# Differential q, k, v as twelve feature-major tiles of the dense stage ahead of the RWKV scan, in place of token-major products beside it

## The chip, the cores and the metric

One core of a Trainium2 chip runs the whole kernel. The metric is the device time of one execution in microseconds (us); the figure for a kernel is the median of its runs.

## The reference, cut to what matters

Two layers run over 640 tokens (512 latent tokens on a grid 64 wide, 128 context tokens) with 1024 features. The first layer mixes tokens by MLA and a retention, the second by differential attention and a bidirectional RWKV-7 recurrence; a gated feed-forward network with a short convolution follows each. The change is in the second layer:

```python
def odd_inputs(h, po):
    w_in, qn, kn = po[:3]
    b, n, _ = h.shape
    dq, dk, dv, p = split_cols(h @ w_in, ODD_SIZES)
    q = rms_norm(dq.reshape(b, n, DIFF_HEADS, 2, DIFF_DH), qn)
    k = rms_norm(dk.reshape(b, n, DIFF_HEADS, 2, DIFF_DH), kn)
    v = dv.reshape(b, n, DIFF_HEADS, 2 * DIFF_DH)
    rw = rwkv_inputs(p, *po[5:13])
    return q, k, v, rw
```

Here h is the normalised and modulated input. q, k and v have 512 columns each (4 heads, two maps of 64 features), and the columns p of the recurrence another 1920. Latent q and k are rotated (rotary position code on pairs of neighbouring features); the attention of a head takes two softmax maps, subtracts lambda times the second from the first, and multiplies by v. Keys and values of 256 cached context tokens are read beside the new ones. The normalised k and the v of the context tokens are outputs.

## The kernel before

**Dense products.** A feature-major tile is 128 output features by all tokens. `fm_steps` (line 454) makes one from a weight that is split into a high and a low fp32r part and an input that is split in the same way: three products (hi*hi, hi*lo, lo*hi) for each of 8 slices of 128 input features and each of two halves of the columns, 48 in all, recorded on line 470. The weights come in order from a list of jobs: `pump` loads them on SP's queue four jobs ahead and splits them on ACT (line 414) and DVE (line 415). The normalised input is not formed for these tiles: the final x is scaled by the modulation and split, two more columns carry the shifts (so 642 columns, 322 and 320), and `fm_norm` multiplies each product by the rstd `rb` (line 665) and adds the shift (line 666).

**The dense stage of the odd layer.** `rwkv_in` runs 15 such tiles for the recurrence in the order `RW_ORDER`. After each tile DVE and ACT form the token shift; four tiles are turned to token-major on TensorE (line 1583), four pass through a gate product (line 1534), and `rwkv_kk` makes a head norm of four of them with `head_sums` (lines 770 and 775), `head_rows` (line 794) and `head_bcast` (line 804). Beside eight of the tiles, lines 1552 and 1554 form the normalised h itself, in place in the eight x tiles, in fp32, for the differential q, k, v. The true x was spilled to DRAM before.

**The scan.** `rwkv_scan` handles five groups of a forward and a backward chunk of 128 tokens. `pre` prepares a group (lines 1791 to 1875), `lb` and `lc` solve its triangular leaves (lines 1890 to 1948), `steps` advances the state (lines 1971 to 2014). `weave` emits them together: first `pre(0)`; then `pre(1)` with the leaves of group 0; then, five times, the steps of group g with `pre(g+2)` and the leaves of g+1. Between their events a background stream is advanced; `BG` gives how many of its steps go into each of these seven parts, and `Side.step` lets no TensorE instruction of the stream go ahead of what the main streams issued a few events before. A scheduler of the framework then sets the order on each engine.

**The background stream.** `side_mix` runs `odd_qkv` and then `diff_attn`. `odd_qkv` takes six groups of 256 columns: for each of five token tiles 8 fp32 products of 128x128 by 128x256 (line 1325, two records each) from the stored h and token-major weights of 1 MB a group. The results are copied and squared on ACT, normalised, multiplied by the gain and rotated on DVE and POOL, turned by two transposes (line 1303), split (lines 440 and 444) into one buffer and stored to DRAM. It has 121 steps. `diff_attn` has 176: for each of 4 heads `load` issues 14 transfers on POOL's queue (lines 1424 to 1429); then, for each of 5 query tiles and 2 maps, the scores (line 1442) go into one PSUM buffer, and DVE takes the maximum, ACT the exponential (line 1448); then the maps are combined, transposed (line 1467) and multiplied by v (line 1472).

After the scan, `odd_out` reloads x and runs the output projection.

## Time and profile before

| what | value |
|---|---|
| median of 3 runs | 2074.09 us (2069.32 to 2077.87) |
| span of the profiled execution, first to last instruction | 2059.5 us |
| TensorE busy, share of the span | 1952.7 us, 95% |
| VectorE (DVE) busy | 1253.8 us, 61% |
| ScalarE (ACT) busy | 887.3 us, 43% |
| GpSimd (POOL) busy | 186.5 us, 9% |
| instructions | 36275 |

The span runs from the first to the last instruction on the core; the device time of a run has some more around it. Lines named L are lines of the kernel. PE is TensorE's products, PEld its weight loads, SP the engine that issues most DMAs; a q behind an engine's name is its sequencer. PEclk is the granted clock of TensorE as a share of 2.4 GHz, so 0.50 is 1.2 GHz. Records of products overlap, since they are pipelined, so a sum of their lengths is above the time that the engine was busy.

### The profile page before, as it was taken

How to read it: one execution, taken by the hardware profiler on the slowest of the kernel's cores; microseconds unless marked ns; L12 is line 12 of the kernel's file. 1: busy time of each engine (PE TensorE's matmuls, PEld its weight loads, DVE VectorE, ACT ScalarE, POOL GpSimd, SP SyncE). 2: the span in 40 equal slices, each digit the busy share in tenths (PEclk: the TensorE clock that was granted, in tenths of full speed). 3: DMA queues.
4: the chain of work that ended last, by engine and by line, in shares of the span. 5: the costliest groups of instructions: out<-in, count | busy, mean ns of one | idle time of the engine just before them, and what ended most of it. 6: DMA issues, size and time to landing. Idle time of an engine off the chain costs nothing.

```text
span 2059.5 us, 36275 instructions
## 1 busy us (share of the span) xinstructions
PE 1952.7 (95%) x14376; PEld 1765.7 (86%) x14376; DVE 1253.8 (61%) x2752; ACT 887.3 (43%) x1680; POOL 186.5 (9%) x365
## 2 busy tenths in 40 slices
PE   6999999999999999999989897898779999999999
PEld 3998565999899899999978676777679999999999
DVE  6554657556456465577436856877667764656555
ACT  4433344334244243456333334667534542524343
POOL 1001000000000000000024332332110000000000
PEclk9999999999999999999989998979989999999999
DMA  8237344234543512143264554454453212122221
GB/s 323 67 109 242 105 134 163 89 104 147 181 153 116 192 62 83 60 151 104 83 207 100 109 161 120 100 116 96 100 200 106 77 58 92 60 85 67 77 63 71
DMA packets 190676, 243.60 MB, mean 118 GB/s; under 512 B 90730, under 2 KB 132970, under 8 KB 190508
## 3 DMA queue, kind: packets, MB, share of 16 engines
q1 hardware_dynamic: 184880, 225.87, 35.7%
q0 software_dynamic: 3904, 13.37, 2.2%
q8 instruction: 113, 1.85, 0.4%
q10 hardware_dynamic: 1724, 2.06, 0.3%
q14 instruction: 55, 0.45, 0.1%
HBM read 202.05 MB, written 39.21 MB: 117 GB/s over the span
## 4 chain that ended last, share of the span: by engine, by line
PE 81%; DVE 7%; DMA 6%; ACT 3%; issue 2%; POOL 1%; SPq 0%; ACTq 0%; DVEq 0%; POOLq 0%
PE mm L470 59%; PE qkv L1325 2%; PE ada L541 2%; PE rv L913 1%; PE pv L1130 1%; PE mm L1097 1%; DMA dk<-pt 1%; PE ptr L1120 1%; PE sc L1442 1%; DVE X L1902 1%; DVE tmp L1901 1%; DMA xd<-X 1%; DMA mq<-tr 1%; DMA raw<-ada 1%; PE mm L1098 1%
## 5 line engine op out<-in xcount | busy, mean ns | idle before, releaser
L414 ACT CAST hi<-raw 128x1024 fp32r<-128x1024 f32 (+4 forms) x212 | 195.9, 925 | 574.1 <-PE mm L470 528.6
L470 PE MATMUL mm<-hhi,hi 128*128 128x322 f32 x1648 | 381.0, 312 | 0.0
L470 PE MATMUL mm<-hlo,hi 128*128 128x322 f32 x1648 | 380.3, 311 | 0.0
L470 PE MATMUL mm<-hhi,lo 128*128 128x322 f32 x1648 | 380.1, 311 | 0.0
L470 PEld LDWEIGHTS mm<-hhi,hi 128*128 128x128 f32 x1648 | 278.3, 189 | 8.7 <-issue 6.7
L470 PEld LDWEIGHTS mm<-hlo,hi 128*128 128x128 f32 x1648 | 279.5, 190 | 0.0
L470 PEld LDWEIGHTS mm<-hhi,lo 128*128 128x128 f32 x1648 | 278.6, 189 | 0.0
L415 DVE TENSOR_TENSOR lo<-raw,hi 128x1024 fp32r<-128x1024 f32 (+4 forms) x212 | 226.1, 1067 | 58.7 <-ACT hi L414 36.0
L672 DVE SCALAR_TENSOR_TENSOR x<-mm,ada,x 128x512 f32<-128x512 f32 (+1 forms) x176 | 88.7, 545 | 176.1 <-PE mm L470 175.9
L470 PE MATMUL mm<-ahi,hi 128*128 128x320 f32 x704 | 161.7, 311 | 0.0
L470 PE MATMUL mm<-ahi,lo 128*128 128x320 f32 x704 | 160.7, 309 | 0.0
L470 PE MATMUL mm<-alo,hi 128*128 128x320 f32 x704 | 160.3, 309 | 0.0
L663 DVE COPY shv<-mm 128x2 f32<-128x2 f32 x103 | 16.3, 159 | 207.9 <-PE mm L470 207.9
L470 PEld LDWEIGHTS mm<-ahi,hi 128*128 128x128 f32 x704 | 117.1, 188 | 12.0 <-ACT hi L414 10.1
L1325 PE MATMUL qkv<-w,x 128*128 128x256 f32 x480 | 118.9, 402 | 0.1
L470 PEld LDWEIGHTS mm<-ahi,lo 128*128 128x128 f32 x704 | 117.8, 188 | 0.0
L470 PEld LDWEIGHTS mm<-alo,hi 128*128 128x128 f32 x704 | 117.6, 188 | 0.0
L666 ACT ACTIVATE u<-u,shv 128x128 f32<-128x128 f32 (+1 forms) x176 | 90.3, 557 | 48.8 <-DVE u L665 47.0
L734 DVE SCALAR_TENSOR_TENSOR ac<-u,vt,ac 128x642 f32<-128x642 f32 x88 | 78.0, 887 | 52.5 <-ACT ac L732 52.3
L1325 PEld LDWEIGHTS qkv<-w,x 128*128 128x128 f32 x480 | 94.0, 201 | 17.0 <-issue 1.7
L732 ACT ACTIVATE ac<-u,vt 128x642 f32<-128x642 f32 x88 | 81.3, 925 | 2.8
L665 DVE TENSOR_TENSOR u<-mm,rb 128x128 f32<-128x128 f32 (+1 forms) x176 | 77.3, 481 | 2.5 <-ACT rb L650 2.5
(419 smaller groups left out, 3351.3 us busy)
## 6 DMA issues: line engine op xcount, KB each, us to landing
raw<-ada SPq DMA_DIRECT2D x96, 512.0 KB, 4.6
raw<-up SPq DMA_DIRECT2D x88, 512.0 KB, 3.5
raw<-down SPq DMA_DIRECT2D x32, 384.0 KB, 3.1
raw<-down SPq DMA_DIRECT2D x32, 320.0 KB, 2.8
fs<-df SPq DMA_DIRECT2D x10, 832.0 KB, 5.2
raw<-wb_fm SPq DMA_DIRECT2D x15, 512.0 KB, 3.5
w<-wb_tm SPq DMA_DIRECT2D x12, 512.0 KB, 4.5
raw<-wa_fm SPq DMA_DIRECT2D x11, 512.0 KB, 4.3
```

Of the source, the lines that this page charges most:

```text
L414: nc.scalar.copy(hi, t)
L415: nc.vector.tensor_tensor(lo, t, hi.bitcast(F32), op=OP.subtract)
L470: nc.tensor.matmul(ps[:, c0 + b:c0 + e], wt[:, ws], at[:, b:e], start=first and j == 0, stop=last and j == 2)
L541: nc.tensor.matmul(ps[32 * j:32 * j + 32, :], self.cs[:, k, :], pieces[j // 2][:, (j % 2) * 512:(j % 2) * 512 + 512], start=k == 0, stop=k ...
L665: nc.vector.tensor_tensor(u[:, o], ps[:, s], rb[:, s], op=OP.mult)
L666: nc.scalar.activation(u[:, o], u[:, o], AF.Identity, bias=sh[:, c:c + 1])
L672: nc.vector.scalar_tensor_tensor(x[:, s], ps[:, s], self.ada_v(l, part, m, c), x[:, s], op0=OP.mult, op1=OP.add)
L732: nc.scalar.activation(ac, u[:, 1:643], AF.Identity, scale=cv[:, 1, f:f + 1], bias=self.vec(f"cb{l}", f))
L734: nc.vector.scalar_tensor_tensor(ac, u[:, 0:642], cv[:, 0, f:f + 1], ac, op0=OP.mult, op1=OP.add)
L913: nc.tensor.matmul(ps[:, :272], at[:, ts], wt[:, k * 272:k * 272 + 272], start=n == 0, stop=n == 23)
L1097: nc.tensor.matmul(sc[:, 0:512], q, kT[:, 0:4], start=True, stop=True)
L1325: nc.tensor.matmul(ps, h[k][:, t * 128:t * 128 + 128], w[k // 4][:, k % 4 * 256:k % 4 * 256 + 256], start=k == 0, stop=k == 7)
```

## The change

The 12 tiles of q, k and v are appended to the list of feature-major weights (`wb_fm` has 27 tiles in place of 15, and `wb_tm` is gone). A new stage `diff_in` runs them after the 15 tiles of the recurrence, from the same split input, with `fm_plain` in place of `fm_norm` (no padding for a token shift). The columns of q and k are permuted inside each head so that the first and second members of the rotary pairs form halves of 32 features; the rotation needs a copy with these halves swapped, made by four DMAs from SBUF to SBUF for each tile. The head norm uses `head_sums`, `head_rows` and `head_bcast`. `odd_qkv`, the normalised copy of h and its lines 1552 and 1554 are removed. The background stream of the scan is the attention alone, and `BG` is set anew. `diff_attn` reads q, k and the cached k in the new layout.

```diff
-BG = (89, 24, 102, 0, 22, 72, 0)
+BG = (14, 24, 26, 26, 26, 30, 30)
...
     def odd_jobs(self):
-        for m in RW_ORDER:
+        for m in RW_ORDER + tuple(range(15, 27)):
             self.jobs_fm("wb_fm", m)
-
-    def odd_qkv(self, D):
...
-                    for k in range(8):
-                        nc.tensor.matmul(ps, h[k][:, t * 128:t * 128 + 128], w[k // 4][:, k % 4 * 256:k % 4 * 256 + 256], start=k == 0, stop=k == 7)
-                        if k % 2:
-                            next(pp, None)
-                            yield
...
     def odd_in(self, hp):
...
-        with self.pool("wd") as wp:
-            self.rwkv_in(D, wp)
+        with self.pool("rbo") as rp:
+            rb = rp.tile([128, TOK], F32, name="rb")
+            with self.pool("wd") as wp:
+                h = self.rwkv_in(D, wp, rb)
+            with self.pool("qk") as qp:
+                self.diff_in(D, h, rb, qp)
         return D
 
+    def fm_plain(self, h, dst, rb):
+
+        nc = self.nc
+        ps = self.fm_tile(h, [8], TOK + 2)
+        sh = self.sp.tile([128, 2], F32, name=self.nm("shv"), tag="shv", bufs=4)
+        nc.vector.tensor_copy(sh, ps[:, TOK:])
+        nc.vector.tensor_tensor(dst, ps[:, :TOK], rb, op=OP.mult)
+        for c, s in ((0, slice(0, LAT)), (1, slice(LAT, TOK))):
+            nc.scalar.activation(dst[:, s], dst[:, s], AF.Identity, bias=sh[:, c:c + 1])
+
+    def diff_in(self, D, h, rb, qp):
...
+        def post(name, ts):
+            sqs = []
+            for t in ts:
+                sqs.append(self.A("qsq", F32))
+                nc.scalar.activation(sqs[-1], t, AF.Square, scale=0.125)
+            yield
+            r = self.head_sums(sqs, 0, self.MM, al)
+            yield
+            rows = self.head_rows(r, self.MM, al)
+            yield
+            for p, t in enumerate(ts):
+                mm = self.head_bcast(rows, p, self.MM)
+                nc.vector.scalar_tensor_tensor(t, t, self.vec(f"d{name}n"), mm, op0=OP.mult, op1=OP.mult)
+                if name == "k":
+                    nc.sync.dma_start(a["dk_o"][p], t[:, LAT:])
+                sw = qp.tile([128, LAT], F32, name=self.nm("sw"), tag="sw", bufs=2)
+                for i in range(4):
+                    j = i ^ 1
+                    nc.sync.dma_start(sw[32 * i:32 * i + 32], t[32 * j:32 * j + 32, :LAT])
+                yield
+                nc.gpsimd.tensor_tensor(sw, sw, rope[:, 1], op=OP.mult)
+                nc.vector.tensor_tensor(t[:, :LAT], t[:, :LAT], rope[:, 0], op=OP.mult)
+                nc.vector.tensor_tensor(t[:, :LAT], t[:, :LAT], sw, op=OP.add)
+                hl = [qp.tile([128, TOK], F32R, name=self.nm("qhl"), tag="qhl", bufs=4) for _ in range(2)]
+                self.split_to(*hl, t)
+                for n in range(2):
+                    nc.sync.dma_start(D[name][p, n], hl[n].bitcast(F32))
+                yield
+
+        pp = iter(())
+        for name in ("q", "k"):
+            ts = []
+            for p in range(4):
+                t = self.A("dq", F32)
+                self.fm_plain(h, t, rb)
+                ts.append(t)
+                for _ in range(3):
+                    next(pp, None)
+            for _ in pp:
+                pass
+            pp = post(name, ts)
+            next(pp)
+        for p in range(4):
+            d = self.A("dv", F32)
+            self.fm_plain(h, d, rb)
+            for _ in range(3):
+                next(pp, None)
...
     def side_mix(self, D):
-        yield from self.odd_qkv(D)
         with self.pool("at", 1, "left") as ap, self.psum("scp") as scp, self.psum("trp") as trp:
             yield from self.diff_attn(D, ap, scp, trp)
...
-            if 1 < n < 10:
-                k = n - 2
-                t = self.x[k]
-                nc.vector.tensor_tensor(t, t, rb, op=OP.mult)
-                for c, s in ((0, slice(0, LAT)), (1, slice(LAT, TOK))):
-                    nc.scalar.activation(t[:, s], t[:, s], AF.Identity, scale=am[:, k, c:c + 1], bias=self.ada_v(1, 0, k, c))
```

Each v tile is then turned to token-major by five transposes and stored, as the recurrence's v is.

## Rows read from the trace of the kernel before

**Rows 1.** The page: the span, and TensorE's granted clock in 40 slices.

```profile
span 2059.5 us, 36275 instructions
...
PEclk9999999999999999999989998979989999999999
```

**Rows 2.** Busy time by stage: stretch, its length, engines with instruction counts, clock, DMA share, GB/s.

```profile
core 0: us, PE busy (x) PEld busy (x) DVE busy (x) ACT busy (x) POOL busy (x), PEclk, DMA share, GB/s
...
968.00:1038.00 70.00, 70.00 (x472) 69.31 (x471) 34.34 (x74) 26.76 (x51) 2.23 (x4) 1.00 0.33 103
...
1291.00:1361.00 70.00, 61.25 (x709) 50.21 (x707) 53.20 (x172) 44.80 (x117) 22.40 (x37) 0.86 0.50 114
...
1050.00:1232.00 182.00, 170.16 (x1027) 137.05 (x1027) 108.87 (x318) 66.54 (x175) 64.38 (x100) 0.92 0.50 125
1232.00:1505.00 273.00, 230.03 (x2900) 189.10 (x2900) 192.94 (x622) 164.27 (x421) 70.35 (x121) 0.86 0.49 117
```

**Rows 3.** Chain that ended last, 968 to 1062: start us, length us, what.

```profile
974.13 0.55 PE mm L794 x5
974.68 7.18 PE mm L470 x48
981.86 0.29 PE mm L804 x2
...
1018.80 0.55 PE vtr L1583 x5
...
1037.57 0.61 PE mm L470 x4
...
1050.55 2.08 PE lp L1800 x8
```

**Rows 4.** Line 1980, a product of every state step: lengths, first and last start.

```profile
L1980 PE MATMUL pa<-G,zb x320: 218/218/366, 1232.0 to 1502.2; 64*64 64x64 f32 x160
```

**Rows 5.** TensorE's groups, 1043 to 1508: count, busy us, mean ns, idle before.

```profile
L1325 PE MATMUL qkv<-w,x 128*128 128x256 f32 x480 | 118.9, 402 | 0.1
L1472 PE MATMUL pv<-av,wT 128*128 128x128 f32 x200 | 35.1, 337 | 1.1 <-ACT wT L1468 1.1
L1442 PE MATMUL sc<-ak,aq 128*128 128x512 f32 (+1 forms) x80 | 32.3, 481 | 19.7 <-ACT p L1448 19.6
...
L1467 PE MATMUL ptr<-ident,p 128*128 128x128 f32 x100 | 21.9, 333 | 4.7 <-ACT wT L1468 2.8 <-ACT wT L1474 1.9
...
L1442 PE MATMUL sc<-ac,aq 128*128 128x256 f32 x64 | 14.7, 316 | 0.0
```

**Rows 6.** Line 1442, the scores: what TensorE sat idle for before them (us, times).

```profile
  ACT p L1448: 42.0, 32
```

**Rows 7.** Chain that ended last, 950 to 1700: token-major products, sums of squares.

```profile
1064.75 7.10 PE qkv L1325 x32
...
1519.43 1.28 PE mm L770 x16
```

**Rows 8.** Chain that ended last, 915 to 968: the head stage of the recurrence.

```profile
962.09 1.05 ACT hi L414
...
966.21 0.76 PE mm L775 x5
```

**Rows 9.** Line 1554, ACT's part of the normalised h: lengths, first and last start.

```profile
L1554 ACT ACTIVATE x<-x,ada,am x16: 478/646/819, 939.9 to 949.8; 128x512 f32<-128x512 f32 x8, 128x128 f32<-128x128 f32 x8
```

**Rows 10.** Timeline of the handover to the scan; idle before and its releaser in brackets.

```profile
1047.85 0.69 SPq L1314 DMA_DIRECT2D w<-wb_tm  x1
1048.54 0.75 ACT L1584 COPY vt<-vtr 128x512 f32<-128x512 f32 x2 [3.87 <-DMA dvt<-vt]
```

**Rows 11.** Weight loads' groups, 1043 to 1232: the token-major products' loads.

```profile
L1325 PEld LDWEIGHTS qkv<-w,x 128*128 128x128 f32 x480 | 94.0, 201 | 17.0 <-issue 1.7 <-ACT m L1333 0.4 <-DMA w<-wb_tm 0.4
```

**Rows 12.** Busy time of line 1442 alone: PE with count, PEld, clock, DMA.

```profile
1429.00:1484.00 55.00, 11.13 (x40) 7.62 (x40) 0.87 0.47 106
1484.00:1505.00 21.00, 0.88 (x4) 0.59 (x4) 0.99 0.68 214
```

**Rows 13.** Busy time in a stretch of the main part, columns as in rows 2.

```profile
1360.00:1370.00 10.00, 9.56 (x165) 8.45 (x166) 4.16 (x14) 7.46 (x19) 2.49 (x5) 0.50 0.34 88
```

More of the change, by code (lines that the diff above doesn't have):

```diff
@@ L32 @@
     ("qn", 1), ("kn", 1), ("qn1", 1), ("kn1", 1), ("retgn", 4), ("diffgn", 4),
[1 row of a table removed]
[1 row of a table added]
 ]
[L35 removed]
+_ROW = [("qnr", 32), ("knr", 32), ("decay", 8), ("lam", 256)]
 _CST = [("cosm", 128), ("sinm", 128), ("reta", 128), ("retb", 128),
@@ L70, in _rope_tables, with _perm_cols, _rope_fm @@
     return lay(c), lay(s)
+PERM = np.concatenate([np.arange(0, 64, 2), np.arange(1, 64, 2)])
+def _perm_cols(w):
+    return w.reshape(w.shape[0], -1, 64)[:, :, PERM].reshape(w.shape[0], -1)
+def _rope_fm():
+    t = np.arange(LAT)
+    inv = 10000.0 ** (-np.arange(16) / 16)
+    ang = np.concatenate([(t // GRID_W)[:, None] * inv, (t % GRID_W)[:, None] * inv], -1).T
+    c, s = np.cos(ang), np.sin(ang)
+    return np.concatenate([np.tile(c, (4, 1)), np.tile(np.concatenate([-s, s], 0), (2, 1))], 1).astype(np.float32)
 def _consts():
@@ L158, in _layout @@
     put("a0", _fm(a["rwkv_a0"][0]))
+    for s in ("q", "k"):
+        put(f"d{s}n", np.tile(a[f"diff_{s}n"][0][PERM], 2)[:, None])
     o["vec"] = vec
     o["row"] = np.concatenate([
-        a["mla_qn"][0][64:], a["mla_kn"][0][64:], a["diff_qn"][0], a["diff_kn"][0],
+        a["mla_qn"][0][64:], a["mla_kn"][0][64:],
         a["ret_decay"][0].reshape(-1), a["diff_lam"][0].reshape(-1)])[None].astype(np.float32)
@@ new lines, in diff_in @@
+    def diff_in(self, D, h, rb, qp):
+        nc, a = self.nc, self.a
+        rope = qp.tile([128, 2, LAT], F32, name="ropd")
+        nc.scalar.dma_start(rope.rearrange("p a t -> p (a t)"), a["ropd"])
+        kc = self.W("kc", 1024)
+        nc.scalar.dma_start(kc, a["dkc"])
+        for n, x in enumerate(self.split_wide(kc)):
+            nc.sync.dma_start(D["kc"][:, n].rearrange("h p x -> p h x"), x.bitcast(F32).rearrange("p (h x) -> p h x", h=4))
+        al = lambda dt: self.A("hr", dt)
+        def post(name, ts):
[44 more added lines that the diff above has]
+                next(pp, None)
+            vt = qp.tile([128, TOK], F32, name=self.nm("dvt"), tag="dvt", bufs=2)
+            for t0, t1 in ((0, 4), (4, 5)):
+                tp = self.PS("vtr")
+                for t in range(t0, t1):
+                    nc.tensor.transpose(tp[:, (t - t0) * 128:(t - t0) * 128 + 128], d[:, t * 128:t * 128 + 128], self.ident)
+                nc.scalar.copy(vt[:, t0 * 128:t1 * 128], tp[:, :(t1 - t0) * 128])
+            cs = slice(p * 128, p * 128 + 128)
+            nc.sync.dma_start(D["v"][:, :, cs].rearrange("t k f -> k t f"), vt.rearrange("k (t f) -> k t f", t=5))
+            nc.sync.dma_start(a["dv_o"][:, cs], vt[:, LAT:])
+        for _ in pp:
+            pass
@@ L1367, in odd_out, with split_wide @@
+    def split_wide(self, src):
+        hi, lo = self.W("khi", 1024, F32R), self.W("klo", 1024, F32R)
+        self.split_to(hi, lo, src)
+        return hi, lo
     def odd_out(self, D):
@@ L1422, in load @@
                 for i in range(2):
+                    src = slice(64 * i, 64 * i + 64)
                     for half in (slice(0, 64), slice(64, 128)):
-                        nc.gpsimd.dma_start(q[i][n][half], D["q"][g, i, 2 * n + y])
-                    nc.gpsimd.dma_start(k[i][rows], D["k"][g, i, 2 * n + y, :, 0:5])
-                nc.gpsimd.dma_start(kc[rows].rearrange("d c t k -> d c (t k)"), D["k"][g, :, 2 * n + y, :, 5:7].rearrange("c d t k -> d c (t k)"))
+                        nc.gpsimd.dma_start(q[i][n][half], D["q"][h, n, src].rearrange("d (t k) -> d t k", t=5))
+                    nc.gpsimd.dma_start(k[i][rows], D["k"][h, n, src].rearrange("d (t k) -> d t k", t=5))
+                nc.gpsimd.dma_start(kc[rows].rearrange("d c t k -> d c (t k)"), D["kc"][h, n].rearrange("(c d) x -> d c x", c=2))
             k = [(k[i], kc[:, i]) for i in range(2)]
@@ L1511, in diff_attn, with rwkv_in @@
         yield from finish(*prev[1])
-    def rwkv_in(self, D, wp):
+    def rwkv_in(self, D, wp, rb):
         nc = self.nc
@@ L1539, in gate @@
             nc.sync.dma_start(D["u"][1, p], vs[p])
-        rb = wp.tile([128, TOK], F32, name="rb")
-        am = self.nx[1]
         h = self.norm_end(us, rb)
@@ L1595, in rwkv_in @@
         gate(3)
+        return h
     def rwkv_kk(self, ks, store, wp):
@@ L2094, in _unpack @@
     sret = r["sret_o"].reshape(2, 64, 2, 2, 128).transpose(2, 3, 0, 1, 4).reshape(1, 1, 2, 4, 64, 128)
-    dk = r["dk_o"].reshape(1, 1, 128, 4, 2, 64)
+    dk = np.empty((128, 4, 2, 64), np.float32)
+    dk[..., PERM] = r["dk_o"].reshape(4, 2, 64, 128).transpose(3, 0, 1, 2)
+    dk = dk[None, None]
     dv = r["dv_o"].reshape(1, 1, 128, 4, 128)
```

91 lines of the change are left out of this document (5 added, 86 removed), and 2 rows, old and new, of the table _VEC.

## The prediction

> **What bounds the kernel now.** I read the views in this order: the page, the busy table by stage, the chain of waits through the odd layer, the groups of TensorE there, and what TensorE's score products waited for. The span is 2059.5 us and the median of the runs 2074.09, so 14.6 us lie outside it; I add the change in us to both [rows 1]. In the whole kernel TensorE is the engine to look at, and only two stages are touched.
>
> The first is the dense stage of the odd layer. From 968 to 1038 TensorE is busy for all of 70 us at full clock, DVE for 34 and ACT for 27 [rows 2]. The chain there is one feature-major tile after another: 48 products in 7.18 us, with the small products of the head sums squeezed between them [rows 3]. What is added here is paid in full, in TensorE time.
>
> The second is the scan. Its first recurrence product that steps a state (line 1980) starts at 1232.0 and its last at 1502.2 [rows 4]. I call 1050.55 to 1232 the prelude (the chunk preparation of two groups and the first leaf solve, with all of q, k, v behind them) and 1232 to 1505 the main part (five groups of steps, with all of the attention behind them). In the prelude TensorE is busy 170 of 182 us, in the main part 230 of 273, or 84% [rows 2]. The background sets the prelude's length: the token-major products have 480 records there and 118.9 us, and end where the steps begin [rows 4, 5]. In the main part the largest stall of TensorE is its own attention: 42.0 us waiting for the exponential that frees the one score buffer [rows 6].
>
> **Part 1, the dense stage: +96 us.** Twelve tiles of the same 48 products cost 12 x 7.18 = 86.2 us [rows 3]. For q and for k there is one head stage each: the sums of squares 1.28 us [rows 7], two sets of five transposes at 0.55, four spreading products at 0.29 [rows 3], together 3.5, for both 7.1. The v tiles need four sets of five transposes, 4 x 0.55 = 2.2 [rows 3]. A head stage can also stall TensorE: the one that is there now did so from 962.09 to 966.21, 4.1 us, behind ACT [rows 8]. The normalised copy of h that ACT made shortly before, 16 pieces of a median 0.646 us or 10.3 us [rows 9], is gone with the change, as are DVE's eight multiplications beside it. I take 1.5 us for each of now three head stages, 4.5 less 4.1, so +0.4; the bounds are 0 and 4.1 a stage, -4.1 and +8.2. Sum 95.9. The vector work of the new tiles (scaling, rope, splits) I cost at nothing: DVE and ACT do 34 and 27 us of 70 in this stage now, 3.5 and 2.8 per tile of 7.18, and may take twice that before TensorE waits. If that cover is gone and each tile takes 2 us longer, it is +24. The swaps of rope halves and the stores of q and k go on SP's queue between the weight loads. Those run four tiles ahead, 29 us of cover, and a swap that is late stops DVE's next addition, then the eviction of a product; three product buffers lie between that and TensorE. I cost them at nothing, up to the same 2 us a tile.
>
> **Part 2, the handover: -6.4 us.** The last dense product ends at 1038.18, the scan's chain begins at 1050.55: 12.4 us [rows 3]. In it the end of v (gate, reversed copy, ten transposes) is still drained, and ACT waits 3.87 us for the store of a transposed v tile [rows 10]; the token-major weight loads are issued just ahead of that. With the change all of this lies under the twelve tiles, and the last tile is a v tile of the attention, which the first scan product doesn't need. New is the first head's load, 14 transfers on POOL's queue with POOL's part of the preparation behind them. I take 6 us of the 12.4, between 4 and 12.4.
>
> **Part 3, the prelude: 181.5 to 97 us.** The removed products issue 32 in 7.10 us, 0.222 each [rows 7], so 480 are 106.5, and the 40 transposes at 0.11 [rows 3] 4.4: 111 of TensorE's 170. There remain 59. The new weave puts 14 + 24 of the 176 attention steps here. Attention's products are 35.1 + 32.3 + 14.7 + 21.9 = 104 us [rows 5]; 38/176 of that is 22.5. So 81.5 us of TensorE work; at the main part's 84% it is 97. Below: 82, no idle time at all. Above: a group of the main part that does preparation, leaf solve and more attention took 70 us [rows 2]; two such are 140. I take 97, nearest to the mixed stretch whose share it uses.
>
> The Trainium skill (Trainium Kernel Development and Optimization, Performance Expectations) says that the busy time of matmuls misleads, since they are pipelined, and that weight loads are the better measure. Here weight loads are busy 137 of 182 us, 94.0 of them for the removed products, and 189 of 273 in the main part [rows 2, 11]; by them, with attention's 22.5 taken as 18 in the main part's proportion of 189 to 230, the prelude is (43 + 18)/0.69 = 88, and the whole sum -31 in place of -22.
>
> **Part 4, the main part: 273 to 246 us.** It loses 38/176 of the attention: of 104 us of products and the 42.0 us of waiting [rows 5, 6] that is 31.5, so 241.5. Against it stands the end. The last stretch of 21 us holds 4 of the 144 score products now, the one before 40 in 55 us [rows 12], or 1.4 us each. The weave sends 30 of 176 steps, some 24.5 score products, into the last group: 34 us at that pace, 13 more than now. Much of that is work taken from the groups before it; I take +5 between 0 and +13. So 246.5. Below: 214, if all of it scales with the attention; above: 286, if the scan's own order sets it and the end is added.
>
> **Sum.** +95.9 - 6.4 - 84.8 - 26.5 = -21.8 us: span 2037.7, median 2052.3. Put otherwise: the scan after its first chain product takes 454.5 us now, the dense part and handover cost 89.5, and the change pays as long as the scan takes less than 365. I expect 343.
>
> **Rivals.** *Slower, by the clock.* The scan keeps about 289 us of busy TensorE at a granted clock of 0.87 (0.92 in the prelude, 0.86 in the main part [rows 2]), 251 us at full clock. At 84% occupancy the scan is 251/(0.843 c) long: 342 at 0.87. What goes out of it is the dense filler that kept TensorE fed; already now there are stretches at 0.50 in the main part, the lower of the two levels [rows 13]. From c = 0.815 down there is no gain; at 0.75 the scan takes 397 and the kernel is 32 us slower, 2106. Against it: the main part holds 0.86 with no token-major product in it. Chance 0.18.
>
> The Trainium skill (TensorE: Matmul & The Clock Gate, HAM oscillation) names this mechanism, that a matmul stream with waits in it falls back to half clock and pays after each wait; the 0.50 stretch agrees with it, and how much more of it the change makes no run here shows.
>
> *No change, the scan's own order.* The main part does not shrink with fewer attention steps because preparation, leaf solve and steps set it: 89.5 + 97 + 273 - 454.5 = +5, 2079. For it: TensorE is busy only 84% there and still a group takes 70 us. Against it: the largest wait is the attention's own. The same time comes out if the dense tiles are 2 us dearer each. Chance 0.24.
>
> *Much faster, the attention sets the main part.* If prelude and main part take their lower bounds of 82 and 214, it is 89.5 + 296 - 454.5 = -69, 2005. For it: the score buffer's wait is the largest one. Against: a last group full of attention, and no idle time left in the prelude. Chance 0.10.
>
> *The forecast*, -22 with a range of its own from -45 to -5: chance 0.48.
>
> **How the numbers follow.** The predicted time is that of the forecast, 2052. The range takes it in, the even case and the near half of the other two: 2018 to 2087. Over 0.5%, or 10 us, is about what a measurement of this kernel can tell from no change. The forecast gives 0.41 to faster and 0.07 to the middle, the much faster case 0.10 to faster; the even case 0.17 to the middle and 0.07 to slower; the clock 0.02 and 0.16. Faster 0.51, same 0.26, slower 0.23.
>
> **What would show it.** Dense tiles at 7.2 us each, 27 of them, and the stage longer by 96; a dearer tile shows DVE or DMA as releaser of its products. The first scan chain product within some 6 us of the last dense one. The first step product about 97 us after that and the last one some 240 later. The score buffer's wait spread over the scan at about the 42 us it has now. A mean clock in the scan of 0.85 or more. The forecast is wrong if the scan takes over 365 us, whether at a lower clock (rival one) or at the same clock with the same group lengths (rival two).

## The result and the profile after

The change makes the kernel slower: 2145.1 us in the median of 4 runs (2139.67 to 2155.46) against 2072.6 for the kernel before beside it, ratio 1.0362 with a 95% interval of 1.0323 to 1.0402. I had forecast 2052.

The page of the kernel after, the lines that answer to [rows 1]:

```profile
span 2145.8 us, 36442 instructions
...
PEclk9999999999999999999988565866879999999999
```

The profiled execution took 2147.5 us, 1.7 more than its span. So only some 2 us lie outside a span: most of the 14.6 us that I put there was the distance between before's profiled execution, a short one, and its median. Between the two profiles the change costs 86 us, between the medians 72.5. Stages are compared by profiles, one of each kernel, and the executions of the kernel after alone lie 16 us apart, so a few us between two stages decide nothing.

Busy time by stage in the kernel after (columns as in [rows 2]): the twelve new tiles, the handover, the prelude, the main part.

```profile
1052.00:1170.00 118.00, 100.70 (x631) 96.64 (x630) 46.47 (x87) 35.53 (x59) 19.08 (x20) 0.90 0.35 107
1170.00:1187.00 17.00, 3.12 (x10) 1.07 (x8) 4.88 (x13) 3.44 (x8) 7.78 (x17) 0.63 0.96 327
...
1187.00:1308.00 121.00, 92.22 (x596) 74.55 (x596) 67.58 (x188) 54.04 (x134) 33.92 (x62) 0.56 0.30 74
...
1308.00:1585.00 277.00, 235.18 (x2770) 192.09 (x2770) 178.44 (x575) 148.55 (x377) 55.75 (x97) 0.74 0.41 90
```

The product of every state step in it, which is the line of [rows 4] under its new number:

```profile
L1989 PE MATMUL pa<-G,zb x320: 218/311/366, 1308.1 to 1584.5; 64*64 64x64 f32 x160
```

| stretch, us | before | after | change | forecast |
|---|---|---|---|---|
| dense stage, from the odd norm's sums to the last dense product | 103.3 | 228.8 | +125.5 | +96 |
| handover, to the first chain product of the scan | 12.4 | 17.1 | +4.8 | -6.4 |
| prelude, to the first state step | 181.5 | 120.7 | -60.8 | -84.8 |
| main part, to the last state step | 270.2 | 276.4 | +6.2 | -26.5 |

All four steps missed on the same side, by 30, 11, 24 and 33 us; some 10 us more are drift ahead of and behind these stages, where the kernels are the same. The granted clock fell from 0.92 to 0.56 in the prelude and from 0.86 to 0.74 in the main part. The typical state product takes 311 ns where it took 218. In the main part TensorE is idle as long as before, 41.8 us of 277 where it was 43.0 of 273 [rows 2]; it is busy 235.2 us where it was 230.0, with 130 records fewer.

Two places of the dense stage, from the timeline of the kernel after (start, length, what; idle before and its releaser in brackets). First the head stage of q; then a product that waits, by way of DVE, for a swap of rope halves:

```profile
1083.28 1.28 PE L788 MATMUL mm<-qsq,c 128*32 128x320 f32 x16
1086.02 0.77 PE L793 MATMUL mm<-ident,hr 128*128 128x128 f32 x5 [1.46 <-ACT hr L790]
1090.09 1.30 PE L812 MATMUL mm<-ident,hr 128*128 128x128 f32 x5 [3.31 <-DVE hr L809]
1092.17 0.90 PE L822 MATMUL mm<-hr,sel 128*128 128x320 f32 x2 [0.78 <-ACT hr L814]
1092.87 0.74 PE L488 MATMUL mm<-hhi,hi 128*128 128x322 f32 x2
...
1096.04 0.46 PE L488 MATMUL mm<-hhi,hi 128*128 128x322 f32 x2
...
1110.02 0.69 DVE L1341 TENSOR_TENSOR dq<-dq,ropd 128x512 f32<-128x512 f32 x1 [3.77 <-DMA sw<-dq]
...
1113.86 0.87 PE L488 MATMUL mm<-hhi,hi 128*128 128x322 f32 x2 [4.18 <-DVE dq L1305]
```

Between two tiles the head stage takes 9.6 us, from 1083.28 to 1092.87, where I had 3.5 of work and 1.5 of stall. It stalls three times, 5.55 us together, and behind it the dense products start every 0.53 us a pair for 3.2 us, not every 0.30: the lower of the two levels of the clock. The k stage repeats the second and third stall, from 1134 to 1140. The swap's stall at 1113.86 is followed by 5.5 us at half clock. The Trainium skill (TensorE: Matmul & The Clock Gate, HAM oscillation) describes this, a product stream that waits and then runs cold, and the trace agrees: 0.53 us a pair behind the 4.18 us wait, too.

The chain of the handover and of the first preparation in the kernel after (start, length, what):

```profile
1169.60 3.82 DMA dk<-qhl
...
1176.70 6.97 DMA wx<-dwd
...
1187.45 2.08 PE lp L1809 x8
...
1198.33 2.00 PE sa L1867 x8
...
1216.23 2.07 PE lp L1809 x8
```

And in the kernel before, the first small load of its handover (timeline), busy time of that handover (columns as in [rows 2]), and a block of products of its first preparation (chain):

```profile
1038.75 1.17 SPq L1678 DMA_DIRECT2D wx<-dwd  x1
...
1038.00:1050.00 12.00, 6.64 (x27) 3.93 (x25) 4.66 (x12) 6.18 (x15) 2.64 (x9) 0.76 0.96 305
...
1063.67 1.08 PE sa L1858 x8
```

The scan's first small load takes 6.97 us in a stretch where the DMA engines are 0.96 busy with stores of k and v and the loads of the attention. They were 0.96 busy in before's handover, too. What differs is when the load is issued: 0.6 us behind the last dense product before (it landed in 3.6), 6.4 us behind it after, with a wait of 3.82 us for a store of k in the chain ahead of it. The block of eight products L1867 takes 2.00 us; its counterpart in before's chain, L1858, takes 1.08.

### The profile page after: what moved, and what is told of

Read it like the earlier page. It is cut to its first block, busy times and chain, and to the rows that moved or that the text cites. A ratio compares the mean times of both kernels' runs of the same rounds, so it can differ in the third digit from the quotient of the medians.

```text
span 2145.8 us, 36442 instructions
## 1 busy us (share of the span) xinstructions
PE 1995.2 (93%) x14520; PEld 1815.1 (85%) x14520; DVE 1249.5 (58%) x2688; ACT 897.9 (42%) x1658; POOL 172.8 (8%) x339
## 5 line engine op out<-in xcount | busy, mean ns | idle before, releaser
L432 ACT CAST hi<-raw 128x1024 fp32r<-128x1024 f32 (+4 forms) x224 | 208.9, 934 | 614.9 <-PE mm L488 569.2
L488 PE MATMUL mm<-hhi,hi 128*128 128x322 f32 (+1 forms) x1840 | 429.9, 315 | 7.0 <-DVE dq L1305 4.2
L488 PE MATMUL mm<-hhi,lo 128*128 128x322 f32 (+1 forms) x1840 | 427.6, 313 | 0.0
L488 PE MATMUL mm<-hlo,hi 128*128 128x322 f32 (+1 forms) x1840 | 425.5, 313 | 0.0
L488 PEld LDWEIGHTS mm<-hhi,hi 128*128 128x128 f32 x1840 | 313.5, 191 | 16.3 <-issue 14.2
L488 PEld LDWEIGHTS mm<-hlo,hi 128*128 128x128 f32 x1840 | 314.3, 191 | 0.0
L488 PEld LDWEIGHTS mm<-hhi,lo 128*128 128x128 f32 x1840 | 314.2, 192 | 0.0
L433 DVE TENSOR_TENSOR lo<-raw,hi 128x1024 fp32r<-128x1024 f32 (+4 forms) x224 | 243.1, 1086 | 50.6 <-ACT hi L432 31.6
L752 DVE SCALAR_TENSOR_TENSOR ac<-u,vt,ac 128x642 f32<-128x642 f32 x88 | 78.1, 888 | 52.9 <-ACT ac L750 52.6
L683 DVE TENSOR_TENSOR u<-mm,rb 128x128 f32<-128x128 f32 (+1 forms) x176 | 77.5, 482 | 2.5 <-ACT rb L668 2.5
L753 DVE SCALAR_TENSOR_TENSOR ac<-u,vt,ac 128x642 f32<-128x642 f32 x88 | 77.9, 885 | 1.4
L488 PE MATMUL mm<-ohi,hi 128*128 128x320 f32 x256 | 59.8, 317 | 2.1 <-DVE ada L568 1.6
```

What stands on the lines that cost most here:

```text
L432: nc.scalar.copy(hi, t)
L433: nc.vector.tensor_tensor(lo, t, hi.bitcast(F32), op=OP.subtract)
L488: nc.tensor.matmul(ps[:, c0 + b:c0 + e], wt[:, ws], at[:, b:e], start=first and j == 0, stop=last and j == 2)
L683: nc.vector.tensor_tensor(u[:, o], ps[:, s], rb[:, s], op=OP.mult)
L752: nc.vector.scalar_tensor_tensor(ac, u[:, 0:642], cv[:, 0, f:f + 1], ac, op0=OP.mult, op1=OP.add)
L753: nc.vector.scalar_tensor_tensor(ac, u[:, 2:644], cv[:, 2, f:f + 1], ac, op0=OP.mult, op1=OP.add)
```

## The experiments

"Scan" is the time from the first chain product (`lp`) to the last start of the state product, read from the first and last starts of these lines as in [rows 4]; clock and TensorE's busy time are those of a window over it. Each run has its own executions of before beside it, with medians from 2066.4 to 2075.2; the ratio is to those.

| run | median, us | ratio to before | scan = prelude + main | clock | TensorE busy |
|---|---|---|---|---|---|
| before | | | 451.7 = 181.5 + 270.2 | 0.89 | 398 |
| after | 2145.1 | 1.0362 | 397.1 = 120.7 + 276.4 | 0.69 | 327 |
| e1_no_attn | 2081.5 | 1.0042 | 347.5 = 104.9 + 242.6 | 0.55 | 274 |
| h3_before_no_attn | 2030.3 | 0.9793 | 425.0 = 183.9 + 241.1 | 0.74 | 368 |
| f8_quarter | 2051.1 | 0.9925 | 435.9 = 139.1 + 296.8 | 0.73 | 368 |
| f5_v_only | 2116.5 | 1.0231 | 459.8 = 148.9 + 310.9 | 0.76 | 402 |
| f6_pt_half | 2091.2 | 1.0101 | 468.9 = 192.0 + 276.9 | 0.86 | 412 |
| e2_fill | 2161.9 | 1.0413 | 415.8 = 123.0 + 292.8 | 0.84 | 357 |
| f1_warm | 2142.6 | 1.0350 | 418.5 = 136.0 + 282.5 | 0.85 | 403 |
| g1_thin | 2267.4 | 1.0915 | 534.0 = 166.6 + 367.4 | 0.52 | 510 |
| g2_fill_back | 2185.6 | 1.0533 | 435.9 = 131.0 + 304.9 | 0.86 | 397 |
| g3_early | 2137.4 | 1.0294 | 405.1 = 134.7 + 270.4 | 0.69 | 336 |
| e3_no_swap | 2145.9 | 1.0352 | 404.3 = 129.3 + 275.0 | 0.67 | 334 |
| e4_ilv | 2145.6 | 1.0340 | 412.8 = 131.6 + 281.2 | 0.66 | 339 |
| g4_ilv_q | 2146.0 | 1.0345 | 408.5 = 131.9 + 276.6 | 0.67 | 337 |
| h1_ilv_no_attn | 2065.1 | 0.9981 | 348.0 = 104.9 + 243.1 | 0.57 | 270 |
| h2_ilv_early | 2135.2 | 1.0307 | 414.4 = 136.6 + 277.8 | 0.67 | 347 |

### What the scan costs, and what q, k, v and the attention cost in it

**e1_no_attn** and **h3_before_no_attn** take the attention out of after and of before (`side_mix`; its outputs o are set to zero).

```diff
-        with self.pool("at", 1, "left") as ap, self.psum("scp") as scp, self.psum("trp") as trp:
-            yield from self.diff_attn(D, ap, scp, trp)
+        for h in range(4):
+            on = self.X("on")
+            self.nc.gpsimd.memset(on, 0.0)
...
```

> The changed kernel with the attention left out (its outputs are zeros): the scan has no background at all. It asks what the scan takes by itself. Theory 'own order' (preparation, leaf solve and state steps set the main part, the low clock only follows): the main part stays within 20 us of its 276 us and the kernel gains at most 30 us. Theory 'TensorE at a low clock' (the time is TensorE's work over its clock at 84% occupancy): a third of TensorE's work in the scan goes, so the scan falls from 397 us by 60 to 120 us even if the clock falls further.

> The kernel before with the attention left out (its outputs are zeros) and q, k, v as they are. Beside e1_no_attn (scan 348 without either) it gives the price of the whole token-major q, k, v in the scan when no attention stands behind it. By my prediction's part 3 they cost their 111 us of TensorE: scan 450, kernel 2060. By the clock (80 us of these products taken from the kernel before gave 15) some 30 to 50: scan 380 to 400, kernel 1990 to 2010.

Prelude and main part of e1_no_attn, and of h3_before_no_attn behind it:

```profile
1183.00:1288.00 105.00, 73.05 (x512) 59.33 (x513) 52.64 (x149) 42.53 (x102) 26.98 (x44) 0.50 0.31 82
1288.00:1530.00 242.00, 200.47 (x2408) 169.73 (x2406) 128.83 (x392) 107.22 (x262) 36.93 (x59) 0.57 0.36 77
```

```profile
1052.00:1236.00 184.00, 171.96 (x1024) 138.68 (x1024) 108.96 (x318) 66.14 (x175) 63.74 (x99) 0.91 0.46 125
1236.00:1477.00 241.00, 196.05 (x2410) 165.50 (x2412) 124.64 (x377) 106.00 (x258) 38.44 (x61) 0.61 0.42 101
```

With nothing behind it the scan takes 347.5 us. My forecast of 343 with the whole attention in it was less than that. Neither theory of e1_no_attn has it: the scan falls by 50 us, not 60 to 120, but the main part by 34, not under 20, and the kernel gains 64, not 30. Four kernels make a table of the scan: bare 347.5, with q, k, v 425.0, with the attention 397.1, with both 451.7. So q, k, v cost 77.5 us without the attention and 54.6 with it, of 111 us of products; h3_before_no_attn's 425 lies between its two expectations and bears out neither. The attention costs 49.6 without q, k, v and 26.7 with them. The main part, 241 and 243 in the kernels without attention, is 270 in before with all 176 steps: 29/176 or 0.17 us a step, where my part 4 had 0.83. In after it is 34 us longer than bare with some three quarters of the steps in it, 0.26 us each.

**f8_quarter** keeps two of the eight products of each token-major tile of before; **f5_v_only** moves only v into the dense stage, as four feature-major tiles, with q and k left in the scan and `BG` set for the shorter stream; **f6_pt_half** gives the transposed q and k of before two half buffers in place of one.

```diff
                     for k in range(8):
+                        if k in (3, 7):
-                        nc.tensor.matmul(ps, h[k]..., start=k == 0, stop=k == 7)
+                            nc.tensor.matmul(ps, h[k]..., start=k == 3, stop=k == 7)
```

```diff
-        for m in RW_ORDER:
+        for m in RW_ORDER + tuple(range(15, 19)):
...
-            for g in range(6):
+            for g in range(4):
```

```diff
-                    pts = tile("pt", 512, 1, F32R).rearrange("p (n x) -> p n x", n=2)
+                    for i in range(2):
+                        pts = tile("pt", 256, 2, F32R).rearrange("p (n x) -> p n x", n=2)
```

> The kernel before, with two of the eight products of each q, k, v tile (three quarters of these products, 80 us of TensorE at full clock, are left out, so q, k and v are wrong); loads, post-processing and stores stay. Theory 'TensorE's products set the prelude': it falls from 182 to about 105 us and the kernel by 70 to 80 us. Theory 'own order and low clock': the prelude falls to 120 at best, as in the changed kernel, at a lower granted clock, and the main part is not shorter: a gain of 40 to 60 us. Theory 'post-processing of q and k': the prelude stays above 150.

> The kernel before, with only v moved ahead as four feature-major tiles; q and k stay token-major beside the scan, and the normalised copy of h with them. The dense stage should be 31 us longer (4 x 7.18 and four sets of transposes). Theory 'the filler's own length sets the prelude' (TensorE and the post-processing of q, k, v): the prelude falls by a third of 182 us at most and by 36 us (160 x 0.222) at least, so -5 to -30 us in all. Theory 'own order, with q, k, v as a filler that fits in': the prelude falls by under 20 us, so the kernel is 10 to 30 us slower than before.

> The kernel before, with the split q and k going through two half-size buffers in place of one (each transposed tile is split and stored in two pieces, twice as many transfers). Theory 'the post-processing of q and k sets the prelude' (47 us of the chain there wait for the store that frees the one buffer): the prelude falls by 15 to 40 us. Theory 'TensorE's products or the scan's own order set it': within 8 us of 182.

Prelude and main part of f8_quarter, then the main part of f5_v_only:

```profile
1053.00:1192.00 139.00, 108.39 (x637) 79.62 (x638) 101.24 (x287) 59.50 (x159) 58.73 (x92) 0.65 0.51 132
1192.00:1489.00 297.00, 259.96 (x2889) 211.91 (x2890) 204.02 (x637) 167.77 (x431) 70.12 (x127) 0.77 0.49 112
...
1237.00:1548.00 311.00, 270.62 (x2845) 218.82 (x2845) 208.02 (x645) 162.45 (x415) 69.06 (x126) 0.71 0.42 97
```

Three quarters of 106.5 us of products are gone in f8_quarter, 80 us, and the scan is 15.8 shorter. The prelude gives 42 of them; the main part, whose TensorE instructions are all but the same (2889 against 2860), takes 27 back, at 0.77 in place of 0.86 [rows 2]. A little of that is spill: the shorter prelude leaves 20 of the 120 records of q, k, v to the main part, where they take 7.6 us. The second theory has the direction (a prelude above 120, a lower clock, a main part that isn't shorter) but not the gain, 15 us in place of 40 to 60; the other two, a prelude of about 105 or above 150, fail.

In f5_v_only, TensorE is busy 402 us with 3684 products, where before's 3885 took 398, at 0.76 in place of 0.89: the scan grows by 8 us though a third of q, k, v has left it. Its prelude falls by 33 us and its main part, with no product of q, k, v in it in either kernel, grows by 41. TensorE is idle there 40 us of 311 where it was 43 of 273 [rows 2]: the added time is all busy time of the same products, at 0.71 in place of 0.86. With the dense stage 34 us longer the kernel is 2.3% slower (interval 1.9 to 2.7), more than either theory allowed.

In f6_pt_half the wait for the one buffer, whose transfers (`dk<-pt` and `dq<-pt`) are 13.9% and 6.2% of before's chain from 1050 to 1232, didn't pay to remove: with twice as many transfers, prelude and main part are 10 and 7 us longer, and the kernel 1.0% (0.6 to 1.4). The prelude is within neither expectation.

### The clock or the order of the scan

**f1_warm** puts 300 useless dense products behind the bare scan of e1_no_attn, **g1_thin** 900 small ones in the same places (its diff is against f1_warm); **e2_fill** puts 160 dense ones behind the scores of after, **g2_fill_back** 240 where the token-major products had been. All but e2_fill set `BG` for the added steps.

```diff
+            for _ in range(300):
+                w = wmp.tile([128, 512], F32, name=self.nm("warm"), tag="warm")
+                self.nc.tensor.matmul(w[:, :256], self.on[:, :128], self.on[:, 128:384], start=True, stop=True)
+                yield
```

```diff
-                self.nc.tensor.matmul(w[:, :256], self.on[:, :128], self.on[:, 128:384], start=True, stop=True)
+                for _ in range(3):
+                    self.nc.tensor.matmul(w[:64, :64], self.on[:64, :64], self.on[:64, 128:192], start=True, stop=True)
```

```diff
+                for _ in range(4):
+                    nc.tensor.matmul(sc[:, 768:1024], q[c][0][:, qt], q[c][0][:, 0:2], start=True, stop=True)
```

```diff
+            for _ in range(120):
+                w = wmp.tile([128, 512], F32, name=self.nm("warm"), tag="warm")
+                for _ in range(2):
+                    self.nc.tensor.matmul(w[:, :256], self.ident, self.rt[:, 0:256], start=True, stop=True)
+                yield
```

> The changed kernel without the attention, as before, and with 300 useless fp32 products of 128x128 by 128x256 as the scan's background (133 us at full clock), spread over its parts. The scan by itself took 348 us at granted clocks of 0.50 and 0.57. Theory 'low clock': with the clock at 0.9 the scan's own chain is shorter, about 300 us in all, although TensorE has 133 us more to do. Theory 'own order' (the chain is DVE, DMA and waits, the clock doesn't matter): 348 us or longer, up to 400.

> The kernel after with the attention left out (its outputs are zeros) and 900 useless products of 64x64 fp32 in the background, three where f1_warm had one dense product of 128x256: about the same TensorE time (six records at 0.07 us, which is what the recurrence products take at the lower clock, are 0.42 us, against 0.444), but few columns. The scan of the run without attention took 348 us, with the dense products 419, so 61 of their 133 us vanished. Theory A (the clock): the dense products paid part of their time back by holding the clock, and these don't: the clock in the scan stays under 0.6, at most 30 of 126 us vanish, the scan takes 443 us or more and the kernel some 2175. Theory B (own order, no effect of the clock on the chain): what vanished lay in waits of TensorE, and these vanish in the same waits: scan 412, kernel 2140.

> The changed kernel with useless work added: behind each of the 40 score products four fp32 products of 128x128 by 128x256 into unused columns of the score buffer, 160 x 0.444 = 71 us at full clock. Theory 'low clock': the granted clock in the scan rises from 0.56 and 0.74 to 0.9 or more, and the scan takes no longer than its 397 us, perhaps 380, with 71 us more work. Theory 'own order': the scan takes longer, 410 to 470 us.

> The kernel after with 240 useless fp32 products of 128x256 (106.6 us at full clock, the size and the place of the token-major products of the kernel before) put back ahead of the attention in the background. Theory A (the clock): they raise the clock of the prelude from 0.56 to 0.85 or more and cost little: 80 us of them taken out of the kernel before gave 15, 71 us put behind the scores cost 17, so scan 397 to 422 and the kernel 2170. Theory B (own order): 29 us of TensorE's idle time in the prelude take them in, the rest is paid: scan 475, kernel 2223.

The whole scan in a window: f1_warm, then g1_thin.

```profile
1179.00:1598.00 419.00, 403.42 (x3515) 280.95 (x3515) 180.59 (x539) 149.01 (x359) 66.32 (x109) 0.85 0.28 64
```

```profile
1178.00:1712.00 534.00, 510.35 (x4674) 434.87 (x4675) 181.61 (x541) 150.11 (x362) 67.64 (x109) 0.52 0.24 53
```

One dense product is two records of 0.222 us [rows 7], so 300 are 133 us: they lengthen the bare scan by 71 (the medians of the kernels differ by 61), at 0.85. That is above the ranges of both theories, some 300 us or 348 to 400 for the whole scan. The 900 small ones, by their expectation 126 us, lengthen it by 187, at 0.52: theory A's bound of 443 us or more holds, though its kernel time of some 2175 is 92 us short, and theory B's 412 doesn't. How much of TensorE's time goes to the added products alone, in f1_warm and then in g1_thin, and the whole window of the bare scan, e1_no_attn:

```profile
1179.00:1598.00 419.00, 208.47 (x585) 105.78 (x585) 0.85 0.28 64
...
1178.00:1712.00 534.00, 236.98 (x1752) 201.03 (x1752) 0.52 0.24 53
...
1183.00:1530.00 347.00, 273.51 (x2914) 229.06 (x2915) 181.47 (x541) 149.75 (x362) 63.90 (x103) 0.55 0.35 79
```

Records are counted to their modelled ends, so these figures are rough. The small products were dearer than expected: 0.135 us a record, not 0.07. What remains of the busy time belongs to the scan's own products. It is 273.5 us bare, 273.4 with the small ones added and 195.0 with the dense ones, while TensorE's idle time falls from 73.5 us to 23.7 and 15.6. So there are two effects. The waits take in 50 to 58 us of any product, and so far theory B is right. The other 79 us that the dense ones get back, and the small ones don't, are the scan's own products running shorter: that is the clock, 0.85 against 0.52.

TensorE is busy 510 of 534 us in g1_thin. The Trainium skill (TensorE: Matmul & The Clock Gate, HAM oscillation) lays the low clock to waits between products; in g1_thin hardly any are left and the clock stays at 0.52, so here the measurement shows more than the Trainium skill does. The stretch at 0.50 of [rows 13] was a sign of it: TensorE is busy for 9.56 of its 10 us.

The same exchange with the attention there: 71 us of dense products in e2_fill cost the scan 18.7, with the clock from 0.69 to 0.84. So the clock rose, but the scan of 415.8 lies in the range of "own order" and not at the 397 or less of "low clock". Of the 106.6 us of g2_fill_back, 97 run in the scan (44 of the 480 records come ahead of it) and cost 38.8, nearer to theory A (25) than to B (78), and outside A's range. Its prelude:

```profile
1189.00:1320.00 131.00, 127.57 (x835) 99.06 (x835) 62.23 (x169) 43.70 (x104) 30.03 (x50) 0.96 0.21 50
```

It is only 10 us longer than after's, with 239 more product records in it: 328 are added ones, and the attention's have all moved to the main part. In all, one us of dense products in the scan costs 0.20 (f8_quarter, taken out), 0.26 (e2_fill), 0.40 (g2_fill_back) or, without the attention, 0.53 us (f1_warm). The whole of q, k, v, with normalisation and stores, costs 0.49 us for each of their 111 with the attention and 0.70 without. In the dense stage a us costs a whole one.

### The attention's place

**g3_early** changes only `BG` of after.

```diff
-BG = (14, 24, 26, 26, 26, 30, 30)
+BG = (60, 60, 14, 14, 14, 14, 0)
```

> The kernel after with the attention earlier in the background: 120 of its 176 steps before the first state step, not 38. My prediction's part 4 (0.83 us of the main part for each attention step): the main part loses 68 us and the prelude gains about as much, less what its 29 idle us take in: the kernel 2125 to 2145. Theory A (the clock): prelude's clock up to 0.75 or more, main part's down to 0.6, so the main part loses less than 50 and the whole comes out the same within 15 us. Theory B (own order): the main part stays at 276 +- 10, the prelude grows by 40 or more, the kernel 2185.

The score products (lines that write `sc`) in the main part of after, then of g3_early:

```profile
1308.00:1585.00 277.00, 33.07 (x106) 23.09 (x106) 24.35 (x29) 25.64 (x56) 0.74 0.41 90
...
1316.00:1587.00 271.00, 21.44 (x66) 13.94 (x65) 15.44 (x19) 16.70 (x38) 0.68 0.41 98
```

`BG` moves 82 attention steps ahead of the first state step, but by the trace only 10 of the 40 score tiles change sides (29 to 19 in DVE's column), a quarter of the attention or 44 steps. For these part 4 would take 37 us off the main part; it gets 6 shorter, and the prelude 14 longer. They run at 0.70 (prelude) and 0.68 (main part), between what theory A forecast (0.75 or more, 0.6) and the clocks of after. The main part agrees with theory B, the prelude and the kernel don't. The kernel is 2137.4, ratio 1.0294 (1.0264 to 1.0325): within theory A's 15 us of after, and within part 4's range too, so the time alone doesn't tell them apart; the 6 us do.

### The dense stage and the handover

**e3_no_swap** leaves the swaps of rope halves out; **e4_ilv** advances the head norm's steps, its sums now in two of them, between the eight slices of the next tile's products, not between tiles; **g4_ilv_q** moves the loads `wx` to ACT's queue on top of that.

```diff
-                for i in range(4):
-                    j = i ^ 1
-                    nc.sync.dma_start(sw[32 * i:32 * i + 32], t[32 * j:32 * j + 32, :LAT])
...
-                nc.gpsimd.tensor_tensor(sw, sw, rope[:, 1], op=OP.mult)
+                nc.gpsimd.tensor_tensor(sw, t[:, :LAT], rope[:, 1], op=OP.mult)
```

```diff
-                self.fm_plain(h, t, rb)
+                self.fm_plain(h, t, rb, pp, AT[p])
...
-                for _ in range(3):
-                    next(pp, None)
```

```diff
-                nc.sync.dma_start(wx[0:64], D["wd"]...)
+                nc.scalar.dma_start(wx[0:64], D["wd"]...)
```

> The changed kernel without the 32 transfers that swap the halves of q and k (the rotation is computed with the halves unswapped; all vector work stays). Theory 'swap transfers' (late swaps stop DVE, then the eviction of a product, and keep SP's queue busy at the handover): the dense stage ends 10 to 20 us earlier and the handover falls from 17 to about 8 us, 20 us in all. Theory 'head stage' (TensorE has nothing to do between two tiles while the sums of squares go through ACT, DVE and back): under 8 us in all.

> The changed kernel with the steps of the head norm and rotation issued inside the next tiles' products in place of between them, the sums, the transposes and the spreading at different points. Nothing is left out. Theory 'head stage': the two stalls of some 5.5 us and the stretches at 1.2 GHz after them (3 us each) go, 12 to 20 us in all. Theory 'swap transfers': under 8 us, since each swap is as late as before.

> The kernel of e4_ilv (head-norm steps spread over the dense tiles) with the loads of the decay inputs wx on ACT's queue, not on SP's behind the stores of q, k and v. If the handover hangs on SP's queue: 20.8 us becomes 12 or less. If on the DMA engines themselves (busy 0.98 there): 18 or more. If what the dense stage saves stays saved, the kernel comes to 2120; if the scan gives it back as in e4_ilv, to 2145.

Without swaps the dense stage ends 7 us earlier, with the steps spread 20 earlier, measured from the first rstd transposes of each kernel, as the profiles differ by some us ahead of it. Without swaps the handover is 14.3 us, not 8, so e3_no_swap gains about 10 us there, between its two theories, and no time in the end (2145.9). The new tiles of e4_ilv leave TensorE 2 us idle in 97, where after had 17 in 118:

```profile
1050.00:1147.00 97.00, 94.95 (x618) 87.20 (x616) 45.40 (x86) 34.51 (x56) 15.52 (x16) 1.00 0.35 108
```

So 20 of the 30 us that part 1 missed are the stalls of the head norm and of the swaps, and the half clock behind them. The kernel gains nothing from it: the handover grows from 17.1 to 21.6 (to the last dense product's end; 20.8 in g4_ilv_q's expectation is to the copy of its shifts) and the scan from 397 to 413. With `wx` on ACT's queue the handover is still 20.2, in g4_ilv_q:

```profile
1149.00:1168.00 19.00, 2.81 (x7) 1.03 (x7) 7.53 (x14) 3.18 (x7) 9.73 (x19) 0.60 1.02 302
```

and in its chain and its timeline:

```profile
1148.29 10.29 DMA dv<-dvt
...
1158.82 0.50 ACTq L1713 DMA_DIRECT2D wx<-dwd  x1
...
1164.20 2.05 PE L1826 MATMUL wp<-wup,wx 65*128 65x512 f32 x2 [12.41 <-DMA wx<-dwd]
```

So SP's queue alone doesn't set it. On the other queue the load is issued some 10 us behind the last dense product all the same, 0.2 us after a store of v has landed that took 10.29, and takes 5 us more while the DMA engines are full. Whether that store holds the issue back wasn't tried. The attention's loads aren't needed for it: without the attention the handover is 16.5 us in e1_no_attn and 17.0 in h1_ilv_no_attn.

**h1_ilv_no_attn** is e4_ilv without the attention, **h2_ilv_early** e4_ilv with g3_early's `BG`.

> The kernel of e4_ilv (head-norm steps spread over the dense tiles, 19 us off the dense stage) with the attention left out (its outputs are zeros), to be read beside e1_no_attn (2081, scan 348). If the 19 us go because the scan's own start hangs on something the dense stage doesn't set, they go here too: 2081. If they go because the attention's steps fall on a scan at the lower clock, they stay here: 2062.

> The kernel of e4_ilv with the attention earlier in the background (120 of 176 steps ahead of the first state step, as in g3_early, which gained 8 us on the kernel after). If an earlier attention holds the clock of the prelude, part of the 19 us of the dense stage stays: 2120 to 2130. If what is saved ahead of the scan is given back in any case: 2137.

Without the attention 16 us stay saved (2081.5 to 2065.1) and the scan is as long as before it, 348.0. With an earlier attention 2135.2, within 3 us of g3_early: given back again. So the scan gives the time back only where the attention's steps are woven into it. The profile shows TensorE busy longer with the same products (339 us for 3352 in e4_ilv, 327 for 3366 in after) at 0.66 in place of 0.69. That the clock is the whole of it is argued, not shown; TensorE's idle time there is 74 us against 71.

## Why the prediction was wrong, step by step

**Part 1, +96, measured +125.5.** With the head stages woven in (e4_ilv) it is 105.9, 10 us above the forecast, so the products were priced about right. The step that failed is "1.5 us for each of now three head stages", with a bound of 4.1, and swaps "at nothing": a head stage that nothing is woven into takes 9.6 us, and each of the three longest stalls (3.31, 4.18 and 3.32 us) is followed by products at half clock. The credit for the old stall was misread, too. Of its 4.1 us TensorE was idle for 1.9 only, as the sums of squares ran in it, and 1.26 of that is left after the change:

```profile
963.83 1.26 PE L770 MATMUL mm<-ksq,c 128*32 128x320 f32 x10 [0.80 <-ACT ksq L1605]
966.21 0.76 PE L775 MATMUL mm<-ident,hr 128*128 128x128 f32 x5 [1.12 <-ACT hr L772]
```

**Part 2, -6.4, measured +4.8.** I counted what leaves the handover, but of what enters it only POOL's queue. The failed step is "With the change all of this lies under the twelve tiles": it does, but the twelve tiles have an end of their own, stores of k and v behind the last product, and I put that at nothing. The scan's first load is issued 5.8 us later than before and lands in 6.97 us in place of 3.6. The DMA engines were as full before (0.96). Why the issue comes late stays open: e4_ilv and g4_ilv_q have it on two queues, and it is late on both.

**Part 3, 181.5 to 97, measured 120.7.** Both halves of "81.5 us of TensorE work; at the main part's 84%" failed. The work was priced at before's clock of 0.92 and takes 92.2 us at 0.56, 11 more; a block of products takes 2.00 us in place of 1.08. And TensorE is busy 76% of the time, not 84%: 28.8 us idle where the forecast left 15.5, 13 more. Bare, the preparation takes 104.9 us at 0.50, with TensorE busy for 73 of them, so the 97 with attention in it couldn't be reached at this clock. The 88 that weight loads gave is farther off still. What the idle time would be at a higher clock isn't shown.

**Part 4, 273 to 246, measured 276.4.** The failed step is "It loses 38/176 of the attention": 0.83 us a step against 0.17 to 0.26 by the runs without attention. I had read the 42.0 us of [rows 6], the largest wait, as time of which a share would be saved. After the change TensorE waits for the exponential only 13.4 us, and the main part is no shorter. TensorE is idle elsewhere instead, 41.8 us in all against 43.0, and with 130 records fewer it is busy for 5 us longer, at 0.74:

```profile
  ACT p L1464: 13.4, 17
```

**The rivals.** The sign of being wrong that I had set, a scan of over 365 us, came: 397.1. Two rivals came true together. The main part didn't shrink, as in "the scan's own order"; and the clock fell as in "slower, by the clock", below its point of no gain of 0.815, to 0.69. That rival's formula gives 431 us for the scan at 0.69 against 397 measured: it has TensorE busy for 251/0.69, or 364 us, and 327 were measured, so not all of the busy time stretches with the clock. Both gave too little, +5 and +32, because neither had the 40 us that dense stage and handover cost beyond the forecast. The rival by the clock held against itself that the main part keeps 0.86 without token-major products in it; the main part of f5_v_only, 0.71 with the same products behind a thinner prelude, shows that this was no proof.

What stays open: how long the scan would be at full clock without any filler, as every run that raised the clock did it with more products; what makes the handover's first load late; and why the attention gives back what the dense stage saves. No version here beats the kernel before with all of its work in it: f8_quarter, the only faster one that keeps the attention (0.9925, interval 0.9896 to 0.9953), leaves products out.

## What to carry to other kernels

Before moving dense products out of a stage that waits on a chain, take the background out of it altogether and time the bare stage: here 348 us of the 452 that it takes, and none of the 17 kernels came below that. Products that fill waits and hold the granted clock cost there a fifth to a half of their time (the whole of q, k, v, with what hangs on it, half to 0.7), while a stage that is bound by TensorE charges them in full. The better direction may be the opposite one, dense products into the scan; no run here tried it. And a wait that stands largest in the list is not time to be had: price a step of the background by a run without it.

## What was unexpected in the hardware

- TensorE at 0.52 of its clock while busy 510 of 534 us (g1_thin), and at 0.85 when busy 403 of 419 with dense products in the same places (f1_warm).
- Nearly the same instructions at three clocks: the main part takes 270 us at 0.86, 297 at 0.77 (f8_quarter) and 311 at 0.71 (f5_v_only), with product records within 1% and TensorE idle for 37 to 42 us in each.
- A 32 KB load that lands after 6.97 us when the DMA engines are 0.96 busy, at the point where the whole scan waits for it; in before's handover, at the same share, it landed after 3.6.
